# A hybrid attention and RWKV layer on one core: where the norm of half 0 keeps its tiles, and what is ordered around it

## The chip, the core and the metric

The kernel runs on one core of a Trainium2 chip. The core has a matrix engine (TensorE, called PE in the profile; PEld are its weight loads), a vector engine (DVE), a scalar engine for activations (ACT), a general engine (POOL) and a queue engine (SP) that issues the DMAs of this kernel, one after the other. The metric is the device time of one execution in microseconds (us); of several runs the median counts. Before the change it was 1794.25 us, the median of 3 runs (1792.09 to 1794.7).

## What is computed

One layer for 1024 tokens of width 1024 in fp32. Two branches, an attention with compressed, selected and windowed keys and an RWKV7 recurrence, are each projected back to width 1024, gated and added; the sum goes through an output projection onto the residual. Then comes a feed-forward block with a causal convolution of width 3 over the tokens between its two projections. Cut to what matters here:

```python
def reference(x, ...):
    h = _rms_norm(x, norm_mix[l])
    u = h @ w_in[l]
    ...
    gates = sigmoid(merge).reshape(B, S, 2, D)
    y = gates[:, :, 0] * (o_nsa @ proj_nsa[l]) + gates[:, :, 1] * (o_rwkv @ proj_rwkv[l])
    x = x + y @ w_out[l]
    x = x + _conv_ffn(_rms_norm(x, norm_ffn[l]), ffn_up[l], ffn_conv[l], ffn_down[l])

def _conv_ffn(h, w_up, conv_w, w_down):
    u = h @ w_up                                # 1024 -> 2 * 2816
    u = causal_depthwise_conv(u, conv_w)        # width 3
    a, b = jnp.split(u, 2, axis=-1)
    return (silu(a) * b) @ w_down
```

## The kernel before

Channels lie on the 128 partitions and tokens along the free axis, in two halves H[0] and H[1] of 512 tokens, so a tile is 128 x 512. A width of 1024 is eight tiles. Every fp32 operand of a large product is split into a high and a low part that the matrix engine takes as fp32r; a product of two operands is three matmuls (high by high, high by low, low by high). `wload` (L233) loads a weight tile as `wraw`, ACT copies the high part to `whi` (L240), and DVE subtracts for `wlo` (L242); there are two buffers each. `mm3` (L245) runs the three matmuls for each of `nk` tiles into one PSUM bank, one at a time (L250); `mm3s` (L254) does so for several products that share the right side (L268).

A tile framework orders the instructions of each engine. It takes them by priority, by and large in the order in which the program issues them, and lets later work of another buffer pass where an earlier one would wait; `tc.cur_priority` shifts a stretch of code back, and `tc.issue_after(i)` keeps an instruction behind instruction `i`. Each engine then runs its list strictly in order, SP's DMA issues too.

Half 0 is finished first. While the RWKV recurrence still runs, a list of dense pieces fills the matrix engine. Its tail is: `rproj` (the gated products of half 0, eight), `yprep` (splits of y), `wout0(m)` for m = 0 to 7 (L749, the output projection of half 0: 24 matmuls into bank psP; residual tile `xr` from the input, named "zs" in the profile, added at L755, stored to `x2_d` at L756, squared on ACT at L761), `norm0` (L766: two matmuls with ones that sum the squares, L770 and L771; Ln and Exp at L774 and L775; then eight tiles are loaded again from `x2_d`, scaled at L780, copied to the high part at L781 and subtracted to the low part at L782), and `ffn0(i)` for i below NEW, the FFN groups of half 0 in the plain form. A group is one 128-wide slice of both halves of `w_up`: two products of 24 matmuls. The pool "f" has three buffers of tag "zs" (NZS) and three of "fu", which the residual tiles, the squares, the reloads and other tiles share.

Half 1 follows, with later priority. `gated((m,), 1, ...)` for m = 0 to 7 makes the gated products (12 matmuls each into bank psB at L250; tanh of the gate `s` at L716; eviction at L720 on DVE; addition to y at L721 on POOL), then come splits of y (L1344, L1345), the output projection of half 1 (`project`, 24 matmuls into psA each), its norm (L1371 to L1382), with the half-0 groups i = NEW to NE - 1 as cover, and the plain FFN groups of half 1 for i below NE. Beside these, `tprep` (L1418) forms T1 to T4, sums and differences of normed tiles of the two halves (split at L1427 and L1428); `TSTEPS[i]` says which tiles' steps are issued after group i. The remaining groups, i = NE to 21, compute both halves and both slices at once as a 2 by 2 block product with seven products instead of eight (`prod`, L1528; 84 matmuls a group in place of 96). In that loop DVE builds weight sums (L1484, L1485, L1489, L1490), u2 and q from PSUM (L1557, L1562), further sums (L1565, L1570, L1574), the convolution taps (L1397, L1399) and the two multiplications of silu (L1406, L1407). FFN down ends the program.

Of the kernel before, what the change touches and what calls it, by code (L numbers as in the profile page):

```python
# [7 lines left out]
F32 = mybir.dt.float32  # L8
FR = mybir.dt.float32r
# [49 lines left out]
NE = 7  # L59
# [3 lines left out]
NEW = 5  # L63
TSTEPS = [(0,), (0, 0), (1, 1), (1, 2), (2, 2), (3, 3), (3,)]
PFD = 3
DSEQ = "nnsnsnsn"
CW = -0.5 * float(np.exp(-0.5))
# [83 lines left out]
def build(tc, D, dbg=None, upto=99):  # L151
# [7 lines left out]
    with ExitStack() as ctx:  # L159
# [84 lines left out]

        def mm3(ps, whi, wlo, xhi, xlo, nk, first=0):  # L245
            n = 0
            early = [(k, a, b) for k in range(first) for a, b in ((whi, xhi), (whi, xlo), (wlo, xhi))]
            for k, a, b in early + [(k, whi, b) for k in range(first, nk) for b in (xhi, xlo)] + [
                    (k, wlo, xhi) for k in range(first, nk)]:
                T.matmul(ps, a[:, k], ks_(b, k), start=(n == 0), stop=(n == 3 * nk - 1))  # L250
                n += 1
                yield

        def mm3s(prods, xhi, xlo, nk, lol=0):  # L254
# [10 lines left out]
            for k in range(0 if lol else nk):  # L265
# [445 lines left out]
        def gated(ms, h, hi, lo, s1, yt, pool_=None):  # L711
            ws, pj = [], []
            for m, s_ in zip(ms, s1):
                ws.append(wload(D["p_rwkv"][m], 4, pool_))
                load(s_, sg_d[8 + m][:, H[h]])
                ltanh[0] = A.activation(s_, s_, AF.Tanh, scale=0.5).ins  # L716
                pj.append(ps("PB"[h]))
            yield from mm3s(list(zip(pj, ws)), hi, lo, 4, LOL[1]) if len(ms) > 1 else mm3(pj[0], *ws[0], hi, lo, 4)
            for p_, s_, y_ in zip(pj, s1, yt):
                V.scalar_tensor_tensor(s_, s_, 1.0, p_, op0=ALU.add, op1=ALU.mult)  # L720
                G.tensor_add(y_, y_, s_)  # L721
# [27 lines left out]
        def wout0(m):  # L749
            hi, lo = wload(D["w_out"][m], 8)  # L750
            xr = FP["f"].tile([128, 512], F32, name="zs", bufs=NZS)
# [4 lines left out]
            nc.sync.dma_start(x2_d[0][m], xr)  # L756
            if m == 0:
# [8 lines left out]
        def norm0():  # L766
# [9 lines left out]
            hi, lo = ktiles(FP["h"], "hhi"), ktiles(FP["h"], "hlo")  # L776
            for k in range(8):
                t = FP["f"].tile([128, 512], F32, name=("fu", "zs")[k % 2], tag=("fu", "zs")[k % 2], bufs=(3, NZS)[k % 2])
                load(t, x2_d[0][k])
                V.scalar_tensor_tensor(t, t, P("norm_ffn", k), rs, op0=ALU.mult, op1=ALU.mult)  # L780
                A.activation(hi[k], t, AF.Copy)  # L781
                V.tensor_sub(lo[k], t, hi[k].bitcast(F32))  # L782
            ob["h2"] = hi, lo
# [3 lines left out]
        def ffn0(i, tags="PP", gate=None, evac=None):  # L787
# [8 lines left out]
            if not i:  # L796
                yield from mm3s(list(zip(pjs, ws)), *ob["h2"], 8, LOL[2])
# [1027 lines left out]
```

## Time and profile before

| | us |
|---|---|
| median of 3 runs | 1794.25 |
| the profiled execution | 1796.17 |
| its span in the trace | 1794.40 |
| PE busy | 1746.9 (97%) |
| DVE busy | 1239.4 (69%) |
| ACT busy | 864.1 (48%) |
| POOL busy | 482.0 (27%) |

The profiled execution is 1.77 us longer than the span that the trace covers, and 1.92 us longer than the median. The page of the profile has the busy time of each engine, the span in 40 slices (each digit tenths of a slice; the granted TensorE clock in tenths of full speed), the chain of work that ended last, and the costliest groups of instructions. The trace behind it gives single instructions: start, duration, engine, source line, operation, output <- inputs, shape, count, and in brackets the idle time of the engine ahead of the instruction and what released it. Matmuls overlap: the step from one start to the next, not the duration, is what one costs. The same holds in part on DVE and ACT.

### The profile page before, as it was taken

To read this page: it belongs to the slowest core of one execution; us is meant where nothing else is said; L and a number is where in the kernel's file an instruction comes from. 1 tells how busy PE (TensorE), PEld (TensorE's weight loads), DVE (VectorE), ACT (ScalarE), POOL (GpSimd) and SP (SyncE) were. 2 spreads that over 40 slices of the span, in tenths; PEclk is the share of its full clock that TensorE was granted. 3 is DMA by queue.
4 is the path that set the end of the run, shared out by engine and by line. 5 is a ranking of instruction groups with operands and counts; after the bars stand their busy time and mean duration, and the time that the engine had idled before them with its cause. 6 is when DMAs were issued, how large, how long until landed. Compare 5 with 4: busy or idle time off the path is not lost.

```text
span 1794.4 us, 30743 instructions
## 1 busy us (share of the span) xinstructions
PE 1746.9 (97%) x11849; PEld 1361.3 (76%) x11860; DVE 1239.4 (69%) x2171; ACT 864.1 (48%) x1572; POOL 482.0 (27%) x358
## 2 busy tenths in 40 slices
PE   8999999999999999999999889999999999999998
PEld 5885657676777778887777768878888888888886
DVE  6224666888776538765446475479998998876799
ACT  5234665757656654545545454355433433524330
POOL 1101031011121120000003130110454444657756
PEclk9998999999999999999999989999999999999999
DMA  6415143232344446445455663443322222524402
GB/s 193 118 53 164 54 157 108 69 110 72 109 155 140 130 141 199 137 124 160 141 159 174 232 217 118 135 145 123 114 88 89 82 77 88 204 102 130 129 13 106
DMA packets 132578, 227.03 MB, mean 127 GB/s; under 512 B 24912, under 2 KB 53968, under 8 KB 132176
## 3 DMA queue, kind: packets, MB, share of 16 engines
q1 hardware_dynamic: 132432, 225.07, 38.9%
q8 instruction: 93, 1.52, 0.4%
q14 instruction: 53, 0.43, 0.1%
HBM read 156.24 MB, written 63.96 MB: 123 GB/s over the span
## 4 chain that ended last, share of the span: by engine, by line
PE 77%; DVE 10%; DMA 5%; ACT 3%; issue 2%; POOL 1%; SPq 1%; ACTq 0%; DVEq 0%; POOLq 0%
PE psP L250 24%; PE psM L1528 7%; PE psA L1528 4%; PE psP L1528 4%; PE psA L250 4%; PE psP L268 3%; PE psB L250 2%; PE psM L250 2%; PE psA L1638 1%; PE psM L1638 1%; PE psA L444 1%; PE psB L1638 1%; PE psP L1638 1%; PE psA L583 1%; DVE pl L594 1%
## 5 line engine op out<-in xcount | busy, mean ns | idle before, releaser
L250 PE MATMUL psP<-hhi,whi 128*128 128x512 f32 x608 | 247.3, 407 | 2.7 <-DVE qn L354 1.4
L250 PE MATMUL psP<-hlo,whi 128*128 128x512 f32 x608 | 242.6, 399 | 0.5 <-DVE hlo L227 0.5
L242 DVE TENSOR_TENSOR wlo<-wraw,whi 128x1024 fp32r<-128x1024 f32 (+1 forms) x100 | 114.3, 1146 | 99.7 <-ACT whi L240 49.5
L250 PE MATMUL psP<-hhi,wlo 128*128 128x512 f32 x608 | 164.8, 402 | 0.0
L240 ACT ACTIVATE whi<-wraw 128x1024 fp32r<-128x1024 f32 (+1 forms) x100 | 95.1, 954 | 111.6 <-PE psP L250 56.4
L594 DVE TENSOR_TENSOR pl<-pf,ph 128x512 f16<-128x512 f32 (+3 forms) x208 | 113.1, 556 | 35.6 <-ACT pf L593 35.0
L250 PEld LDWEIGHTS psP<-hhi,whi 128*128 128x128 f32 x608 | 114.4, 188 | 29.3 <-ACT ad L892 1.6
L250 PEld LDWEIGHTS psP<-hlo,whi 128*128 128x128 f32 x608 | 114.4, 188 | 25.8 <-issue 2.1
L592 ACT ACTIVATE ph<-psA 128x512 f16<-128x512 f32 (+3 forms) x208 | 99.2, 477 | 65.7 <-PE psA L587 39.4
L250 PEld LDWEIGHTS psP<-hhi,wlo 128*128 128x128 f32 x608 | 112.0, 188 | 24.1 <-issue 0.5
L535 DVE TENSOR_REDUCE mp<-psM 128x1 f32<-128x512 f32 (+1 forms) x192 | 95.7, 516 | 32.8 <-PE psM L533 18.4
L593 ACT ACTIVATE pf<-psA 128x512 f32<-128x512 f32 (+3 forms) x208 | 99.6, 479 | 0.0
L1464 POOL TENSOR_TENSOR wlo<-wraw,whi 128x1024 fp32r<-128x1024 f32 (+1 forms) x31 | 63.2, 2040 | 125.4 <-DVE s L1490 59.4
L602 PEld LDWEIGHTS <-pl 128*128 128x128 f16 x592 | 55.0, 98 | 20.6 <-DVE pl L594 6.9
L616 POOL TENSOR_TENSOR onat<-onat,ot 128x256 f32<-128x256 f32 x32 | 24.5, 771 | 171.8 <-DVE ot L615 152.6
L597 PEld LDWEIGHTS <-ph 128*128 128x128 f16 x592 | 55.7, 96 | 19.4 <-issue 8.0
L1264 POOL TENSOR_TENSOR b<-b,bonus 128x512 f32<-128x512 f32 x8 | 10.4, 1294 | 205.1 <-ACT b L1262 151.9
L1407 DVE SCALAR_TENSOR_TENSOR th<-th,u 128x512 f32<-128x512 f32 x37 | 64.6, 1747 | 0.5
L1463 ACT ACTIVATE whi<-wraw 128x1024 fp32r<-128x1024 f32 (+1 forms) x37 | 32.8, 887 | 63.5 <-issue 26.8
L600 PEld LDWEIGHTS <-ph 128*128 128x128 f16 x592 | 56.1, 97 | 3.7 <-issue 3.0
L1464 POOL TENSOR_TENSOR s34l<-s,s34h 128x1024 fp32r<-128x1024 f32 x15 | 36.3, 2423 | 74.7 <-ACT s34h L1463 74.5
L1464 POOL TENSOR_TENSOR s12l<-s,s12h 128x1024 fp32r<-128x1024 f32 x15 | 37.5, 2497 | 43.1 <-PE psA L1528 31.6
(759 smaller groups left out, 5054.6 us busy)
## 6 DMA issues: line engine op xcount, KB each, us to landing
wraw<-f_up SPq DMA_DIRECT2D x58, 512.0 KB, 3.4
wraw<-w_t SPq DMA_DIRECT2D x46, 512.0 KB, 3.9
wraw<-f_dn SPq DMA_DIRECT2D x22, 512.0 KB, 3.8
th_d<-th SPq DMA_DIRECT2D x37, 256.0 KB, 2.0
sg_d<-zs SPq DMA_DIRECT2D x32, 256.0 KB, 2.9
wraw<-w_out SPq DMA_DIRECT2D x16, 512.0 KB, 3.9
z_d<-zs SPq DMA_DIRECT2D x28, 256.0 KB, 3.0
x<-xT SPq DMA_DIRECT2D x24, 256.0 KB, 5.6
```

The source lines that it names most:

```text
L240: A.activation(hi[:, :nk], raw, AF.Copy)
L242: (V if WK[0] <= wk[0] < WK[1] else G).tensor_sub(lo[:, :nk], raw, hi[:, :nk].bitcast(F32))
L250: T.matmul(ps, a[:, k], ks_(b, k), start=(n == 0), stop=(n == 3 * nk - 1))
L535: V.reduce_max(mp[:, x, br, t:t + 1], pm[:, 0:(b1 - b0) * 128], axis=AX.X)
L592: A.activation(ph[0:nkey, rg], pa[0:nkey, rg], AF.Exp, scale=0.125)
L593: A.activation(pf[0:nkey, rg], pa[0:nkey, rg], AF.Exp, scale=0.125)
L594: V.tensor_sub(pl[0:nkey, rg], pf[0:nkey, rg], ph[0:nkey, rg])
L600: T.matmul(pov[:, t, 0:64], ph[0:nkey, tk], vt[0:nkey, kb, g, 65:129], start=False, stop=False, skip_group_check=True)
L1407: V.scalar_tensor_tensor(th, th, 0.5, ub, op0=ALU.mult, op1=ALU.mult)
L1464: e.tensor_sub(lo[:, ks], raw[:, ks], hi[:, ks].bitcast(F32))
L1528: T.matmul(bank, w[wi][:, o_ + k], xs_[k][xi], start=start and n == 0, stop=n == 11, skip_group_check=True)
L1638: T.matmul(pj, x[:, m], y, start=(n == 0), stop=(n == 5))
```

## The change

Five things change. (1) The residual tiles of `wout0` get buffers of their own in the h pool (tags XT, four of them), and `norm0` works on the tiles of k = 4 to 7 where they lie; only k = 0 to 3 are loaded again. The order of the tiles is NK = 4, 5, 6, 7, 0, 1, 2, 3, in the first FFN group too. (2) On DVE, the scaling of tile n waits for the subtraction of tile n - HL, HL = 2. (3) Of the gated products of half 1, the tanh of m = 7 (GT) stands behind the last copy of the norm, the matmuls of m = 6 and 7 (GD) behind the last matmul of `wout0`, and their evictions (GE) behind the norm's last subtraction. (4) The addition to y runs on DVE instead of POOL for all m of half 1 (GV = 0). (5) NE is 6 instead of 7 and NEW 4 instead of 5: group 6 goes from the plain to the combined form, and `TSTEPS` is spread over six groups.

```diff
--- before.py
+++ after.py
@@ -56,14 +56,23 @@
 GAPS = (1, 1, 3)
 SVP = 20000
 SVI = 1
-NE = 7
+NE = 6
 WV = (3, 99, 1)
 WK = (0, 200)
 LV = 20
-NEW = 5
-TSTEPS = [(0,), (0, 0), (1, 1), (1, 2), (2, 2), (3, 3), (3,)]
+NEW = 4
+TSTEPS = [(0, 0), (0, 1), (1, 1), (2, 2), (2, 3), (3, 3)]
 PFD = 3
 DSEQ = "nnsnsnsn"
+GD = 6
+GT = 7
+GE = 6
+GV = 0
+HL = 2
+NK = (4, 5, 6, 7, 0, 1, 2, 3)
+XT = ("hhi_6", "hlo_5", "hlo_6", "hlo_7")
+HT = ("hhi_4", "hlo_4", "hhi_5", "hhi_0", "hhi_7", "hlo_0", "hhi_1", "hlo_1", "hhi_2", "hlo_2", "hhi_3", "hlo_3", "hhi_6",
+      "hlo_5", "hlo_6", "hlo_7")
 CW = -0.5 * float(np.exp(-0.5))
 LN2 = 0.6931471805599453
 
@@ -242,16 +251,18 @@
             (V if WK[0] <= wk[0] < WK[1] else G).tensor_sub(lo[:, :nk], raw, hi[:, :nk].bitcast(F32))
             return hi, lo
 
+        lastm = [None]
+
         def mm3(ps, whi, wlo, xhi, xlo, nk, first=0):
             n = 0
             early = [(k, a, b) for k in range(first) for a, b in ((whi, xhi), (whi, xlo), (wlo, xhi))]
             for k, a, b in early + [(k, whi, b) for k in range(first, nk) for b in (xhi, xlo)] + [
                     (k, wlo, xhi) for k in range(first, nk)]:
-                T.matmul(ps, a[:, k], ks_(b, k), start=(n == 0), stop=(n == 3 * nk - 1))
+                lastm[0] = T.matmul(ps, a[:, k], ks_(b, k), start=(n == 0), stop=(n == 3 * nk - 1)).ins
                 n += 1
                 yield
 
-        def mm3s(prods, xhi, xlo, nk, lol=0):
+        def mm3s(prods, xhi, xlo, nk, lol=0, ko=None):
             n = 0
             for k in range(nk if lol else 0):
                 for ps_, w_ in prods:
@@ -262,7 +273,7 @@
                 for ps_, w_ in prods:
                     T.matmul(ps_, w_[0][:, k], ks_(xlo, k), start=False, stop=(k == nk - 1))
                     yield
-            for k in range(0 if lol else nk):
+            for k in () if lol else ko or range(nk):
                 for a, b in ((0, xhi), (0, xlo), (1, xhi)):
                     for ps_, w_ in prods:
                         T.matmul(ps_, w_[a][:, k], ks_(b, k), start=(n == 0), stop=(n == 3 * nk - 1))
@@ -713,12 +724,15 @@
             for m, s_ in zip(ms, s1):
                 ws.append(wload(D["p_rwkv"][m], 4, pool_))
                 load(s_, sg_d[8 + m][:, H[h]])
-                ltanh[0] = A.activation(s_, s_, AF.Tanh, scale=0.5).ins
+                with tc.issue_after(ob["nh"]) if h and m >= GT else ExitStack():
+                    ltanh[0] = A.activation(s_, s_, AF.Tanh, scale=0.5).ins
                 pj.append(ps("PB"[h]))
-            yield from mm3s(list(zip(pj, ws)), hi, lo, 4, LOL[1]) if len(ms) > 1 else mm3(pj[0], *ws[0], hi, lo, 4)
+            with tc.issue_after(ob["wl"]) if h and ms[0] >= GD else ExitStack():
+                yield from mm3s(list(zip(pj, ws)), hi, lo, 4, LOL[1]) if len(ms) > 1 else mm3(pj[0], *ws[0], hi, lo, 4)
             for p_, s_, y_ in zip(pj, s1, yt):
-                V.scalar_tensor_tensor(s_, s_, 1.0, p_, op0=ALU.add, op1=ALU.mult)
-                G.tensor_add(y_, y_, s_)
+                with tc.issue_after(ob["nl"]) if h and ms[0] >= GE else ExitStack():
+                    V.scalar_tensor_tensor(s_, s_, 1.0, p_, op0=ALU.add, op1=ALU.mult)
+                    (V if h and ms[0] >= GV else G).tensor_add(y_, y_, s_)
 
         YS = (("fu", "fu"), ("hhi_4", "fu"), ("hhi_5", "yx"), ("hhi_0", "hlo_0"), ("hhi_1", "hlo_1"),
               ("hhi_2", "hlo_2"), ("hhi_3", "hlo_3"), ("hhi_7", "hlo_4"))
@@ -748,12 +762,14 @@
 
         def wout0(m):
             hi, lo = wload(D["w_out"][m], 8)
-            xr = FP["f"].tile([128, 512], F32, name="zs", bufs=NZS)
+            xr = FP["h"].tile([128, 512], F32, name=f"xr{m}", tag=XT[m % 4])
             load(xr, D["xT"][m][:, H[0]])
             pj = ps("P")
             yield from mm3(pj, hi, lo, ob["yh"], ob["yl"], 8, 0 if m else YE)
             V.scalar_tensor_tensor(xr, pj, 0.5, xr, op0=ALU.mult, op1=ALU.add)
             nc.sync.dma_start(x2_d[0][m], xr)
+            ob.setdefault("xr", []).append(xr)
+            ob["wl"] = lastm[0]
             if m == 0:
                 A.activation(ob["sq"], xr, AF.Square)
             else:
@@ -773,14 +789,20 @@
             rs = FP["f"].tile([128, 512], F32, name="rs0", tag="yx")
             A.activation(rs, pss, AF.Ln, bias=epst[:, 0:1], scale=1.0 / 1024)
             A.activation(rs, rs, AF.Exp, scale=-0.5)
-            hi, lo = ktiles(FP["h"], "hhi"), ktiles(FP["h"], "hlo")
-            for k in range(8):
-                t = FP["f"].tile([128, 512], F32, name=("fu", "zs")[k % 2], tag=("fu", "zs")[k % 2], bufs=(3, NZS)[k % 2])
-                load(t, x2_d[0][k])
-                V.scalar_tensor_tensor(t, t, P("norm_ffn", k), rs, op0=ALU.mult, op1=ALU.mult)
-                A.activation(hi[k], t, AF.Copy)
-                V.tensor_sub(lo[k], t, hi[k].bitcast(F32))
-            ob["h2"] = hi, lo
+            hi, lo, los = [None] * 8, [None] * 8, []
+            for n, k in enumerate(NK):
+                hi[k], lo[k] = (FP["h"].tile([128, 512], FR, name=f"h2{c}0_{k}", tag=HT[2 * n + x]) for x, c in enumerate("hl"))
+                if k > 3:
+                    t = ob["xr"][k]
+                else:
+                    t = FP["f"].tile([128, 512], F32, name=("fu", "zs")[k % 2], tag=("fu", "zs")[k % 2],
+                                     bufs=(3, NZS)[k % 2])
+                    load(t, x2_d[0][k])
+                with tc.issue_after(los[n - HL]) if n >= HL else ExitStack():
+                    V.scalar_tensor_tensor(t, t, P("norm_ffn", k), rs, op0=ALU.mult, op1=ALU.mult)
+                ob["nh"] = A.activation(hi[k], t, AF.Copy).ins
+                los.append(V.tensor_sub(lo[k], t, hi[k].bitcast(F32)).ins)
+            ob["h2"], ob["nl"] = (hi, lo), los[-1]
             for _ in range(GAPS[2]):
                 yield "gap"
 
@@ -794,7 +816,7 @@
                     yield from mm3(pjs[o], *ws[o], *ob["h2"], 8)
                     evict(i, o, pjs[o], us[o], evac)
             if not i:
-                yield from mm3s(list(zip(pjs, ws)), *ob["h2"], 8, LOL[2])
+                yield from mm3s(list(zip(pjs, ws)), *ob["h2"], 8, LOL[2], NK)
                 for o in range(2):
                     evict(i, o, pjs[o], us[o], evac)
             uv = us
```

Lines behind the diff move by 22 in the later part of the file: L1528 becomes L1550, L1557 becomes L1579.

The first place is PE around the second sum with ones, at the end of the norm's sums (sq are the added squares, zs the last square, oh and ol the RWKV output of half 1, yh the split y of half 0). Before:

```order
L250 MATMUL psP_12660<-yh6_12379,wlo_12653 128x512
L250 MATMUL psP_12660<-yh7_12383,wlo_12653 128x512
L770 MATMUL psP_12690<-sq0_12387,ones_70 128x512
L771 MATMUL psP_12690<-zs_12687,ones_70 128x512
L268 MATMUL psP_12759<-hhi_0_12696,whi_12753 128x512
L268 MATMUL psP_12767<-hhi_0_12696,whi_12761 128x512
L268 MATMUL psP_12759<-hlo_0_12704,whi_12753 128x512
```

After the change:

```order
L261 MATMUL psB_13248<-oh_13074,whi_13240 128x512
L261 MATMUL psB_13248<-ol_13075,whi_13240 128x512
L261 MATMUL psB_13248<-oh_13074,wlo_13241 128x512 x4
L787 MATMUL psP_12690<-zs_12687,ones_70 128x512
L261 MATMUL psB_13277<-oh_13074,whi_13269 128x512
L261 MATMUL psB_13277<-ol_13075,whi_13269 128x512
```

The second sum stood right behind the first and right ahead of FFN group 0; now gated products of half 1 lie on both sides of it: 24 matmuls between the two sums with ones, and 24 between the second one and FFN group 0.

The second place is DVE in the norm of half 0, from its first scaling (fu, zs and xr are the tiles scaled, hhi or h2h0 their high part). Before:

```order
L780 SCALAR_TENSOR_TENSOR fu_12712<-fu_12712,par_68,rs0_12693 128x512
L780 SCALAR_TENSOR_TENSOR zs_12717<-zs_12717,par_68,rs0_12693 128x512
L780 SCALAR_TENSOR_TENSOR fu_12722<-fu_12722,par_68,rs0_12693 128x512
L780 SCALAR_TENSOR_TENSOR fu_12732<-fu_12732,par_68,rs0_12693 128x512
L780 SCALAR_TENSOR_TENSOR zs_12727<-zs_12727,par_68,rs0_12693 128x512
L782 TENSOR_TENSOR hlo_0_12704<-fu_12712,hhi_0_12696 128x512
L780 SCALAR_TENSOR_TENSOR zs_12737<-zs_12737,par_68,rs0_12693 128x512
L782 TENSOR_TENSOR hlo_1_12705<-zs_12717,hhi_1_12697 128x512
L782 TENSOR_TENSOR hlo_2_12706<-fu_12722,hhi_2_12698 128x512
```

After the change:

```order
L802 SCALAR_TENSOR_TENSOR xr4_12544<-xr4_12544,par_68,rs0_12693 128x512
L802 SCALAR_TENSOR_TENSOR xr5_12582<-xr5_12582,par_68,rs0_12693 128x512
L1367 TENSOR_TENSOR ylo_13070<-yt_13237,yhi_13069 128x512
L804 TENSOR_TENSOR h2l0_4_12697<-xr4_12544,h2h0_4_12696 128x512
L802 SCALAR_TENSOR_TENSOR xr6_12620<-xr6_12620,par_68,rs0_12693 128x512
L804 TENSOR_TENSOR h2l0_5_12702<-xr5_12582,h2h0_5_12701 128x512
L802 SCALAR_TENSOR_TENSOR xr7_12658<-xr7_12658,par_68,rs0_12693 128x512
L804 TENSOR_TENSOR h2l0_6_12707<-xr6_12620,h2h0_6_12706 128x512
L802 SCALAR_TENSOR_TENSOR fu_12718<-fu_12718,par_68,rs0_12693 128x512
L804 TENSOR_TENSOR h2l0_7_12712<-xr7_12658,h2h0_7_12711 128x512
```

Six scalings stood ahead of most subtractions; now a subtraction follows each scaling, two tiles behind, with tiles 4 to 7 first.

The third place is DVE in the combined loop, from u2 of one group to the sum into psB (p1 and q are sums of products, u00 to u11 the four tap tiles of a group). Before:

```order
L1557 TENSOR_TENSOR u2_14962<-psM_14933,p1_14948 128x512
L1407 SCALAR_TENSOR_TENSOR th_14922<-th_14922,u10_14867 128x512
L1562 TENSOR_TENSOR q_14996<-psA_14934,p1_14948 128x512
L1399 SCALAR_TENSOR_TENSOR u11_14868<-psM_14780,par_68,u11_14868 128x2
L1407 SCALAR_TENSOR_TENSOR th_14927<-th_14927,u11_14868 128x512
L1484 TENSOR_TENSOR s12_15151<-wraw_15131 128x512
L1485 TENSOR_TENSOR s12_15151<-s12_15151,wraw_15129 128x512
L1397 SCALAR_TENSOR_TENSOR u00_15018<-psP_14932,par_68,u00_15018 128x511
L1397 SCALAR_TENSOR_TENSOR u00_15018<-psP_14932,par_68,u00_15018 128x510
L1565 TENSOR_TENSOR psB_14935<-psM_14933,q_14996 128x512
```

After the change:

```order
L1579 TENSOR_TENSOR u2_14951<-psM_14922,p1_14937 128x512
L1419 SCALAR_TENSOR_TENSOR u10_14856<-psM_14769,par_68,u10_14856 128x510
L1421 SCALAR_TENSOR_TENSOR u11_14857<-psM_14769,par_68,u11_14857 128x1
L1419 SCALAR_TENSOR_TENSOR u00_15007<-psP_14921,par_68,u00_15007 128x511
L1429 SCALAR_TENSOR_TENSOR th_14911<-th_14911,u10_14856 128x512
L1421 SCALAR_TENSOR_TENSOR u11_14857<-psM_14769,par_68,u11_14857 128x2
L1419 SCALAR_TENSOR_TENSOR u00_15007<-psP_14921,par_68,u00_15007 128x510
L1429 SCALAR_TENSOR_TENSOR th_14916<-th_14916,u11_14857 128x512
L1584 TENSOR_TENSOR q_14985<-psA_14923,p1_14937 128x512
L1587 TENSOR_TENSOR psB_14924<-psM_14922,q_14985 128x512
```

Between u2 and q there stood one multiplication of silu; now both multiplications and the taps of psP and the last of psM stand there, and the weight sums (L1484, L1485) have moved behind.

## The prediction

> **What bounds the kernel now.** I first read the page's part on the span in slices, then busy times by stretch.
>
> ```profile
> PE   8999999999999999999999889999999999999998
> PEclk9998999999999999999999989999999999999999
> 1014.00:1060.00 46.00, 41.20 (x169) 32.82 (x170) 24.27 (x31) 20.41 (x32) 16.07 (x12) 0.96 0.80 280
> 1060.00:1083.00 23.00, 15.68 (x53) 10.76 (x51) 13.52 (x21) 10.56 (x16) 0.76 (x1) 0.78 0.28 91
> 1173.00:1285.00 112.00, 111.40 (x486) 90.89 (x485) 105.46 (x164) 57.26 (x83) 20.11 (x7) 1.00 0.43 141
> 1285.00:1573.00 288.00, 288.00 (x1264) 236.85 (x1263) 258.96 (x371) 121.79 (x175) 142.83 (x69) 1.00 0.31 104
> ```
>
> A stretch row gives its length, the busy time of PE, PE's weight loads, DVE, ACT and POOL (instructions in brackets), the granted clock, the DMA share and GB/s. TensorE is the bound nearly everywhere: in 1285 to 1573, the loop in seven products, it never pauses, but DVE is busy there for 259 of 288 us. The slices have one visible dip, slices 23 and 24; in time, 1014 to 1083, where the half-0 output projection ends, half 0 is normalised and the first FFN group starts. The clock falls there too. The timeline of PE names the gaps:
>
> ```profile
> 1011.96 2.03 PE L250 MATMUL psP<-yh,wlo 128*128 128x512 f32 x8
> 1015.36 0.70 PE L250 MATMUL psB<-oh,whi 128*128 128x512 f32 x2 [1.37 <-issue]
> 1022.06 0.50 PE L250 MATMUL psP<-yh,whi 128*128 128x512 f32 x1 [3.44 <-DVE zs L755]
> 1024.31 0.63 PE L250 MATMUL psP<-yh,whi 128*128 128x512 f32 x1
> 1059.61 1.02 PE L770 MATMUL psP<-sq,ones 128*128 128x512 f32 x2
> 1062.72 1.23 PE L771 MATMUL psP<-zs,ones 128*128 128x512 f32 x2 [2.09 <-ACT zs L761]
> 1067.35 1.22 PE L268 MATMUL psP<-hhi,whi 128*128 128x512 f32 x2 [3.39 <-ACT hhi L781]
> 1069.94 1.22 PE L268 MATMUL psP<-hlo,whi 128*128 128x512 f32 x2 [1.37 <-DVE hlo L782]
> 1082.96 0.50 PE L250 MATMUL psM<-hhi,whi 128*128 128x512 f32 x1 [0.47 <-ACT whi L240]
> 1094.14 10.88 PE psP L250 x48
> ```
>
> The last row is from the chain of waits: 48 matmuls at full clock take 10.88 us, 0.2267 us each. From 1013.99 (the end of the first row, product 4 of the output projection) to 1082.96 (the second FFN group) are 68.97 us. The work in it is 72 matmuls of wout0(5) to (7), 96 of the eight gated products of half 1 and 48 of FFN group 0: 216 x 0.2267 = 49.0, and 2.2 for the two sums with ones. So 17.8 us are lost: the bracketed gaps add up to 1.37 + 3.44 + 2.09 + 3.39 + 1.37 + 0.47 = 12.1, and 5.7 are matmuls at a low clock.
>
> **Term 1, the norm of half 0.** Before, all gated products stand ahead of the end of wout0(7); nothing is left to run while the last residual, its square, the table load, Ln, Exp, scaling and split follow one another. After, 24 matmuls (products 4 and 5) stand between the two sums with ones, and 24 (6 and 7) between the second sum and FFN group 0, each 24 x 0.2267 = 5.44 us. The work is the same; only the losses change.
>
> Gap at the second sum: 2.09 under 5.44 of cover, gone. The norm chain:
>
> ```profile
> 1062.69 1.28 ACT L768 ACT_TABLE_LOAD   x1
> 1063.98 0.63 ACT L1344 ACTIVATE yhi<-yt 128x512 fp32r<-128x512 f32 x1
> 1065.88 0.75 DVE L780 SCALAR_TENSOR_TENSOR fu<-fu,par,rs 128x512 f32<-128x512 f32 x1 [0.55 <-ACT rs L775]
> 1066.66 0.63 ACT L781 ACTIVATE hhi<-fu 128x512 fp32r<-128x512 f32 x1 [0.82 <-DVE fu L780]
> ```
>
> From the end of the second sum (1063.95) to the first FFN matmul are 3.4 us now. The change puts on ACT, between Exp and the first split, a table load (1.28, the tanh of product 6 needs another table), that tanh (0.63) and one split of y, so about 0.5 more that DVE's scaling doesn't hide: 5.8 against 5.44. I take 0.7 with the lag of the second tile; the gap at L782 (1.37) goes, as subtractions alternate with scalings. Bounds: 0 if ACT slips the tanh in while DVE scales, 3.0 if each 128x512 step on ACT lands late. In the Trainium skill, "ScalarE: Activation LUTs", section "What ACT_TABLE_LOAD costs", a drain of about 1.38 us follows each load, which speaks against an added load. This trace shows none: the load at 1062.69 is followed by work at 1063.98, 1.29 later. By that rule the forecast would be an estimated 1785.4.
>
> Start of the stretch. The residual tiles no longer share the three "zs" buffers, so their loads move up in SP's queue and wout0(5) follows wout0(4) without the 1.37. What comes late next is the weight tile of wout0(6):
>
> ```profile
> 1015.98 5.31 DMA zs<-xT
> 1016.65 0.33 SPq L157 DMA_DIRECT2D wraw<-w_out  x1
> 1023.22 1.06 ACT L240 ACTIVATE whi<-wraw 128x1024 fp32r<-128x1024 f32 x1 [0.48 <-DMA wraw<-w_out]
> ```
>
> It is split at 1024.3. wout0(5) and one gated product (36 matmuls) last until 1013.99 + 8.16 = 1022.15: 2.1 idle instead of 3.44 and 1.37. Does a gap of 2.1 cool the clock?
>
> ```profile
> 945.00:950.00 5.00, 2.81 (x34) 1.92 (x32) 2.48 (x6) 1.89 (x3) 0.00 (x0) 0.76 0.55 189
> 947.30 1.02 PE L268 MATMUL psP<-ohi,whi 128*128 128x512 f32 x2 [2.19 <-ACT ohi L704]
> 1015.00:1020.00 5.00, 3.26 (x12) 2.10 (x12) 2.05 (x3) 2.15 (x4) 0.00 (x0) 1.00 1.06 398
> ```
>
> A gap of 2.19 stands at a clock of 0.76, one of 1.37 at 1.00; so yes, and by the row at 1024.31 (0.42 from one matmul to the next) some eight matmuls cost 1.5. The Trainium skill, "TensorE: Matmul & The Clock Gate", section "Part 1: The HAM clock gate", sets the idle window at about 3.4 us. The trace has a low clock beside 2.19; by the rule the 1.5 would fall away and the forecast be an estimated 1782.5.
>
> The loss at 1082.96 (0.5) stays, since the next group's weights wait for the same buffers. For loads that come later in SP's queue (four reloads of x2 fewer, but weights and gates in another order) I add 1.0. Bounds 0 and 5.7, all of today's low-clock loss again, since DMA is at 0.80 in this stretch.
>
> New losses: 2.1 + 1.5 + 0.7 + 0.5 + 1.0 = 5.8 instead of 17.8: **-12.0**, bounds -17.3 (only the 0.5 left) and -5.
>
> The y addition of half 1 moves from POOL to DVE, eight times 0.6. DVE has 24.27 of 46 us busy; the two last evictions wait for the norm's last subtraction, and behind them on DVE stand only splits for matmuls 48 and more later. I cost it at 0; without that cover 1.2.
>
> **Term 2, one FFN group.** A group in both halves takes 96 matmuls plain and 84 combined: -12 x 0.2267 = **-2.7**. PE is bound on both sides, so this counts in full.
>
> **Term 3, the way into the combined loop.** The plain groups of half 1 cover DVE's sums T1 to T4.
>
> ```profile
> 1024.31 1.23 DVE L242 TENSOR_TENSOR wlo<-wraw,whi 128x1024 fp32r<-128x1024 f32 x1 [2.30 <-ACT whi L240]
> 1025.45 0.68 DVE L1334 TENSOR_TENSOR ol<-stg,oh 128x512 fp32r<-128x512 f32 x1
> 1182.14 5.39 DVE L1378 SCALAR_TENSOR_TENSOR hf<-x,par,rstd 128x512 f32<-128x512 f32 x8 [1.12 <-ACT rstd L1373]
> 1272.51 0.39 PE L1528 MATMUL psP<-hhi,whi 128*128 128x512 f32 x1
> 1277.84 0.20 DVE L1399 SCALAR_TENSOR_TENSOR u<-cvl,par,u 128x1 f32<-128x1 f32 x1
> 1279.36 0.67 DVE L1428 TENSOR_TENSOR T2l<-t,T2h 128x512 fp32r<-128x512 f32 x1
> 1280.73 0.39 PE L1528 MATMUL psM<-T2l,s12h 128*128 128x512 f32 x1
> 1284.27 0.50 PE L1528 MATMUL psM<-T2h,s12h 128*128 128x512 f32 x1 [0.60 <-ACT s12h L1463]
> ```
>
> The last T2 tile is done at 1280.03 and used at 1280.73: 0.7 of slack, with DVE busy 105.46 of 112. One plain half-1 group less takes 48 matmuls (10.9) from PE's way there; T2's last tile is wanted seven matmuls later in the loop (+1.6): 9.3 earlier. DVE, by the two orders from the first L1378 to that T2l, loses four taps (0.66), two 1024-wide splits (1.14 from start to start) and four small ones (0.13) and gains two 512-wide (0.60): 4.2. PE waits 9.3 - 4.2 - 0.7 = 4.4, with 0.7 for the clock after it (some four matmuls at 0.42), less the 0.60 that is there now: **+4.5**. Bounds 0 (DVE's 6.5 us of idle time lie where it can use them) and 6.5 (the same again for T1 and T4).
>
> **Sum.** -12.0 - 2.7 + 4.5 = -10.2. The profiled execution took 1796.17 (span 1794.40 and 1.77 around it): 1786.0. It lies 1.9 above the median of the runs shown, 1794.25, so I predict **1784.0**. All good ends give -20 (1774), all bad ones -1.2 (1793).
>
> **Rivals.** *The loop waits for DVE* (the other side). The scheduler also orders the combined groups, sixteen after the change, in another way:
>
> ```profile
> 1438.13 0.68 DVE L1562 TENSOR_TENSOR q<-psA,p 128x512 f32<-128x512 f32 x1
> 1442.26 0.39 PE L1528 MATMUL psA<-h2hi,s34h 128*128 128x512 f32 x1
> 1455.08 2.28 DVE L1407 SCALAR_TENSOR_TENSOR th<-th,u 128x512 f32<-128x512 f32 x1
> ```
>
> q must be read before the h2 product may add to psA: 3.4 us of slack now. After, two taps, two small ones and a second 2.28 us multiply come ahead of q, 4.4 later; the h2 product comes 26 matmuls after T1's end instead of 12, 3.2 later. That leaves 2 us, and DVE is busy there for 258.96 of 288, 17.2 us of a group's 19.1 (84 x 0.2267). For each us that DVE runs later than this, all sixteen groups pay: 16 us. From 0.64 us beyond (10.2 / 16) the kernel is no faster than before; 1 us beyond gives 1784 + 16 = 1800. Against it: nothing is added per group, and PE never waits in this loop now. Chance 0.08.
>
> *Loads bind the norm stretch*: the DMA row for the gates,
>
> ```profile
> s<-sg_d SPq DMA_DIRECT2D x8, 256.0 KB, 5.4
> ```
>
> lands slowly, and products 6 and 7, now last, wait for gates and weights behind SP's queue. Then term 1 gives only 5: 1791. Chance 0.15. Should the gated products at the end only move the wait (the norm starts 5.4 us later), it is the same price.
>
> *No wait at the loop's entry*: DVE uses its idle time, term 3 is 0 or nearly, 1779 to 1780. Chance 0.17. My forecast keeps 0.60.
>
> **How the numbers follow.** The range takes in the forecast, the no-wait rival and most of the load rival: 1776 to 1792. A measurement can tell about 0.2% (3.6 us) from no change. Faster by more than that (under 1790.7): 0.60 + 0.17 and a little of the load rival, 0.80; within it 0.12; slower than 1797.8: 0.08.
>
> **What would show it.** In the changed profile the second sum with ones follows gated matmuls without a gap; FFN group 0 starts with under 1 us idle; the second FFN group comes some 57 us after wout0(4) instead of 69; one gap of about 2 us stands before wout0(6) with ACT's split of w_out behind it; the loop's entry has one PE wait of about 4 us on a T tile from DVE; PE is busy without pause afterwards, 19.1 us a group. Gaps in every group before psA's h2 product, or idle time before products 6 and 7 put down to a DMA, would prove me wrong.

## The result and the profile after

The changed kernel took 1781.18 us (median of 20 runs, 1775.68 to 1794.13) against 1795.39 us of the kernel before in the same series (20 runs, 1785.96 to 1803.52). The ratio is 0.9925, 95% interval 0.9907 to 0.9943; it is estimated from all runs of both kernels, and so differs a little from the quotient of the two medians (0.9921). Two later comparisons of the same kernel gave 0.9936 (0.9913 to 0.9960; medians 1785.49 against 1794.33) and 0.9934 (0.9912 to 0.9956; 1781.15 against 1793.13). 1784.0 was forecast.

The page's two lines on PE in the 40 slices, after:

```profile
PE   8999999999999999999999999999999999999998
PEclk9998999999999999999999999999999999999999
```

The dip in slices 23 and 24 is gone, and in this view so is the low clock beside it; a slice is 44.5 us long and hides a cold stretch of 6 us that is left (see the timeline below). The waits of PE from 980 us on, after (engine, line, releaser; us in all, times, longest):

```profile
PE psP L261 <- ACT whi L249: 4.3, 1, 4.3
PE psP L1660 <- DVE acc L1740: 1.3, 1, 1.3
PE psP L1550 <- ACT p L1576: 1.2, 1, 1.2
PE psM L261 <- ACT whi L249: 1.1, 1, 1.1
PE psM L1550 <- DVE T2l L1450: 0.4, 1, 0.4
```

None of them is in the norm: the waits at the sums and at the first FFN group have left the list. One wait is larger than any before, 4.3 us on a weight split; two small ones stand at the entry of the combined loop. The timeline of PE around the norm, after:

```profile
1023.59 0.80 PE L261 MATMUL psP<-yh,whi 128*128 128x512 f32 x1 [4.30 <-ACT whi L249]
...
1045.81 1.02 PE L786 MATMUL psP<-sq,ones 128*128 128x512 f32 x2
1052.13 1.02 PE L787 MATMUL psP<-zs,ones 128*128 128x512 f32 x2
1058.61 0.73 PE L279 MATMUL psP<-h2h,whi 128*128 128x512 f32 x2
1071.26 0.50 PE L261 MATMUL psM<-h2h,whi 128*128 128x512 f32 x1 [1.12 <-ACT whi L249]
```

The second sum comes 6.3 us after the first and FFN group 0 another 6.5 us later, with no idle time: 24 gated matmuls run in each of these stretches. After the wait of 4.30, 14 matmuls start 0.43 us apart instead of 0.23, up to 1029.72: the clock is low there.

Three lengths serve for all runs below. **w0** is the start of the first matmul of wout0(0). **S** is the time from w0 to the first matmul of the second FFN group, less 29.87, the time from w0 to the end of wout0(4) in the trace before (1013.99 - 984.12). So S is the stretch that the prediction has at 68.97. **E** runs from there to the end of the last matmul; it holds terms 2 and 3. All are read from the start times of single matmuls.

| kernel | w0 | S | E | wait for wout0(6)'s weights | waits at FFN group 0 | ratio to before, 95% interval |
|---|---|---|---|---|---|---|
| before | 984.1 | 69.0 | 707.3 | (3.4 on the residual tile) | 4.8 | 1 |
| changed | 981.1 | 60.3 | 706.7 | 4.3 | 0 | 0.9925, 0.9907 to 0.9943 |
| changed, again | 977.2 | 58.0 | 708.8 | 3.0 | 0.2 | 0.9936, 0.9913 to 0.9960 |
| changed, third | 979.0 | 58.9 | 706.1 | 3.3 | 0.8 | 0.9934, 0.9912 to 0.9956 |
| norm's part alone | 985.8 | 58.7 | 706.8 | 3.6 | 0.3 | 0.9930, 0.9908 to 0.9952 |
| FFN group alone | 977.7 | 71.2 | 707.0 | (3.4 on the residual tile) | 4.3 | 1.0014, 0.9992 to 1.0037 |
| zs buffers, reload | 977.6 | 63.9 | 706.7 | (3.5 on the residual tile) | 2.9 | 0.9978, 0.9958 to 0.9997 |
| no holds | 982.8 | 60.7 | 708.9 | 3.1 | 2.6 | 0.9952, 0.9934 to 0.9971 |
| no lag | 977.2 | 62.1 | 708.1 | 3.0 | 3.7 | 0.9936, 0.9914 to 0.9958 |
| additions on POOL | 984.1 | 60.9 | 706.1 | 3.4 | 1.6 | 0.9951, 0.9933 to 0.9969 |
| x loads late | 979.3 | 53.7 | 708.8 | 0 | 1.4 | 0.9905, 0.9874 to 0.9936 |
| x loads late, second time | 982.7 | 53.4 | 708.8 | 0 | 1.0 | 0.9905, 0.9882 to 0.9929 |
| x and y late | 980.8 | 55.5 | 706.7 | 0 | 1.6 | 0.9927, 0.9903 to 0.9952 |
| first combined product early | 981.5 | 53.7 | 715.2 | 0 | 1.4 | 0.9975, 0.9953 to 0.9997 |

Between the first two traces the span fell by 1794.4 - 1781.9 = 12.5. Of this 8.7 is S and 0.7 is E; 3.0 lie ahead of w0, and 0.1 at the very end. The 3.0 are not the change's: w0 lies anywhere from 977.2 to 985.8, in kernels whose program up to there is the same, and at 981.1, 977.2 and 979.0 in three traces of one and the same kernel.

### The profile page after: what moved, and what is told of

Read it like the earlier page. It is cut to its first block, busy times and chain, and to the rows that moved or that the text cites. A ratio compares the mean times of both kernels' runs of the same rounds, so it can differ in the third digit from the quotient of the medians.

```text
span 1781.9 us, 30738 instructions
## 1 busy us (share of the span) xinstructions
PE 1739.7 (98%) x11837; PEld 1355.8 (76%) x11848; DVE 1240.7 (70%) x2184; ACT 869.4 (49%) x1572; POOL 480.0 (27%) x354
## 4 chain that ended last, share of the span: by engine, by line
PE 78%; DVE 11%; DMA 5%; ACT 3%; issue 2%; SPq 1%; POOL 0%; DVEq 0%; ACTq 0%; POOLq 0%
PE psP L261 24%; PE psM L1550 7%; PE psA L1550 5%; PE psP L1550 5%; PE psA L261 4%; PE psB L261 3%; PE psP L279 2%; PE psM L261 2%; PE psA L1660 1%; PE psM L1660 1%; PE psA L455 1%; PE psB L1660 1%; PE psP L1660 1%; PE psA L594 1%; DVE pl L605 1%
## 5 line engine op out<-in xcount | busy, mean ns | idle before, releaser
L261 PE MATMUL psP<-hhi,whi 128*128 128x512 f32 x560 | 228.7, 408 | 2.7 <-DVE qn L365 1.4
L261 PE MATMUL psP<-hlo,whi 128*128 128x512 f32 x560 | 224.0, 400 | 0.5 <-DVE hlo L236 0.5
L261 PE MATMUL psP<-hhi,wlo 128*128 128x512 f32 x560 | 152.7, 403 | 0.0
L261 PEld LDWEIGHTS psP<-hhi,whi 128*128 128x128 f32 x560 | 105.4, 188 | 27.5 <-ACT ad L914 1.6
L261 PEld LDWEIGHTS psP<-hlo,whi 128*128 128x128 f32 x560 | 105.4, 188 | 24.0 <-issue 1.9
L261 PEld LDWEIGHTS psP<-hhi,wlo 128*128 128x128 f32 x560 | 103.0, 188 | 22.2 <-issue 0.5
L1486 POOL TENSOR_TENSOR wlo<-wraw,whi 128x1024 fp32r<-128x1024 f32 (+1 forms) x33 | 68.0, 2060 | 143.0 <-PE psA L261 46.3
L1429 DVE SCALAR_TENSOR_TENSOR th<-th,u 128x512 f32<-128x512 f32 x38 | 59.6, 1567 | 0.1
L1485 ACT ACTIVATE whi<-wraw 128x1024 fp32r<-128x1024 f32 (+1 forms) x38 | 33.5, 880 | 42.4 <-PE psP L1550 28.6
L1550 PE MATMUL psP<-h2h,whi 128*128 128x512 f32 x128 | 50.1, 391 | 1.2 <-ACT p L1576 1.2
```

Of the source, the lines that this page charges most:

```text
L261: lastm[0] = T.matmul(ps, a[:, k], ks_(b, k), start=(n == 0), stop=(n == 3 * nk - 1)).ins
L1429: V.scalar_tensor_tensor(th, th, 0.5, ub, op0=ALU.mult, op1=ALU.mult)
L1486: e.tensor_sub(lo[:, ks], raw[:, ks], hi[:, ks].bitcast(F32))
L1550: T.matmul(bank, w[wi][:, o_ + k], xs_[k][xi], start=start and n == 0, stop=n == 11, skip_group_check=True)
```

## The experiments

**The norm's part alone.** The changed kernel with the old numbers of groups.

```diff
-NE = 6
+NE = 7
-NEW = 4
+NEW = 5
-TSTEPS = [(0, 0), (0, 1), (1, 1), (2, 2), (2, 3), (3, 3)]
+TSTEPS = [(0,), (0, 0), (1, 1), (1, 2), (2, 2), (3, 3), (3,)]
```

> The changed kernel with NE = 7, NEW = 5 and the old TSTEPS: the norm's part alone. S is the stretch from the end of wout0(4) to the first matmul of the second FFN group, 68.97 us before and 60.31 in the changed kernel. Theory (the norm's part gives most of the gain): S 60 to 61, the wait for wout0(6)'s weights about 4, no gap at the sums; loop entry as before (0.6); the time 8 to 12 below before, ratio 0.9935 to 0.9955. Rival (the 3 us that already separate the two traces ahead of wout0 come from the change too): the same S, but 11 to 13 below before, ratio under 0.9935.

S 58.7, a wait of 3.6, ratio 0.9930, that is 12.5 us of 1792.67 with an interval from 9 to 16. S is a little under what the theory gave. The ratio lies in the rival's range, and its interval takes in the theory's as well. But its trace has w0 at 985.8, later than in the kernel before, so the new norm gains nothing ahead of wout0; and the next run, with the old norm, has w0 at 977.7. The norm's part carries the gain; the rival falls with w0.

**The FFN group alone.** The kernel before with the new numbers.

```diff
-NE = 7
+NE = 6
-NEW = 5
+NEW = 4
-TSTEPS = [(0,), (0, 0), (1, 1), (1, 2), (2, 2), (3, 3), (3,)]
+TSTEPS = [(0, 0), (0, 1), (1, 1), (2, 2), (2, 3), (3, 3)]
```

> The kernel before with NE = 6, NEW = 4 and the new TSTEPS: one FFN group moved to the combined form, the norm untouched. As forecast: 12 matmuls fewer (-2.7), a wait at the loop's entry of 4 to 5: +1.8, ratio 1.001. Theory after the trace (DVE uses its idle time, entry costs about 2.3): -0.4, ratio 0.9998, entry gaps 1 to 2 in all. Rival (the entry costs nothing): -2.7, ratio 0.9985. S stays 69 in all three.

Ratio 1.0014 (0.9992 to 1.0037), E 707.0 against 707.3: the time cannot tell the forecast (1.001) from the theory (0.9998), and the rival's 0.9985 lies just outside. The trace gives -0.3 and one wait at the entry. The timeline of PE and a stretch behind the wait (length, PE, PEld, DVE, ACT, POOL, PEclk, DMA share, GB/s), this kernel:

```profile
1254.17 0.50 PE L1528 MATMUL psP<-hhi,whi 128*128 128x512 f32 x1 [1.22 <-ACT p L1554]
1255.00:1260.00 5.00, 5.00 (x16) 3.93 (x15) 4.97 (x10) 1.75 (x2) 1.08 (x1) 0.66 0.15 57
```

So twelve matmuls fewer (2.7) are nearly given back at the entry: the wait is 0.6 longer than the one there before, and behind it seven matmuls start 0.43 us apart at a low clock, which costs 1.4. In the changed kernel's first trace the same wait of 1.22 stands at the same place, and the clock stays at 1.00. S is 71.2 here where 69 was expected: its gaps are those of the kernel before, 0.4 longer in all (3.0 instead of 2.1 at the second sum), and most of the rest are more matmuls at a low clock.

**Residual tiles in the shared buffers again**, with all eight loaded again. The holds (GD, GT, GE) and the lag (HL) stay.

```diff
-            xr = FP["h"].tile([128, 512], F32, name=f"xr{m}", tag=XT[m % 4])
+            xr = FP["f"].tile([128, 512], F32, name="zs", bufs=NZS)
...
-                if k > 3:
+                if k > 8:
```

> The changed kernel with the residual tiles back in the shared zs buffers and all eight tiles loaded again for the norm; the three holds and the lag stay. Theory (the buffers decide where the gated products stand, and these products are the cover): all eight products run ahead of the sums again, gaps of about 2 at the second sum and about 3 at the first FFN matmul return, S 66 to 70, the whole 6 to 9 slower than the changed kernel. Rival (the holds alone keep two products back, and the lag helps): the gap at the first FFN matmul stays under 1, S 62 to 64.

The timeline of PE, this kernel:

```profile
1008.42 0.70 PE L261 MATMUL psB<-oh,whi 128*128 128x512 f32 x2 [0.97 <-issue]
1015.12 0.50 PE L261 MATMUL psP<-yh,whi 128*128 128x512 f32 x1 [3.45 <-DVE zs L769]
...
1052.70 1.02 PE L786 MATMUL psP<-sq,ones 128*128 128x512 f32 x2
1053.55 1.02 PE L787 MATMUL psP<-zs,ones 128*128 128x512 f32 x2
1057.46 1.22 PE L279 MATMUL psP<-h2h,whi 128*128 128x512 f32 x2 [2.89 <-ACT h2h L803]
```

Neither case as written. The wait ahead of FFN group 0 (2.89) returns, as the theory said, and so does the wait for the residual tile (3.45), which it did not name; but the second sum follows the first at once, since the holds alone keep products 6 and 7 behind wout0, where they cover the last square. S is 63.9, in the rival's band, 3.6 to 5.8 above the changed kernel's three traces and 5.1 under before. So by S the buffers of the residual tiles are worth about half of the gain. By the ratios (0.9978 against 0.9925 to 0.9936) it is more, 7.5 to 9.5 us, but each of these ratios has an interval of some 4 us to either side. The buffers bring 24 of the 48 covering matmuls to their place and start wout0(5) without a wait.

**No holds.**

```diff
-GD = 6
-GT = 7
-GE = 6
+GD = 8
+GT = 8
+GE = 8
```

> The changed kernel with GD, GT and GE = 8, so no hold of the tanh, the matmuls or the evictions of products 6 and 7. Theory (the buffers decide, the holds do little): the products stay where they are on PE, S 60 to 62, the time within 2 us of the changed kernel. Rival (the holds keep DVE and ACT free for the norm): two evictions and two additions (2.4) and a tanh run ahead of the norm's tiles, a gap of 1.5 to 3 at FFN group 0, S 62 to 64.

```profile
1059.39 0.74 PE L279 MATMUL psP<-h2h,whi 128*128 128x512 f32 x2 [1.58 <-ACT h2h L803]
1061.98 0.72 PE L279 MATMUL psP<-h2l,whi 128*128 128x512 f32 x2 [0.19 <-DVE h2l L804]
1064.45 0.73 PE L279 MATMUL psP<-h2l,whi 128*128 128x512 f32 x2 [0.81 <-DVE h2l L804]
```

In this PE timeline the matmuls of the products stand where they did (sums 6.3 apart, FFN group 0 after 24 more), but 1.58 + 0.19 + 0.81 = 2.6 of waits come at FFN group 0, as the rival said. S is in the theory's band all the same; it grows by less (60.7 against 58.0 to 60.3), because the waits ahead of it came out smaller in this trace: 3.1 for wout0(6) and 0.5 for the second group. The holds place no matmul here; what they do is keep DVE and ACT free for the norm's tiles.

**No lag.**

```diff
-HL = 2
+HL = 8
```

> The changed kernel with HL = 8: DVE scales all eight tiles ahead of the first subtraction. Theory (the alternation brings the low parts in time): the first low part comes 6 x 0.66 = 4 later; FFN group 0 takes it as its third matmul, so a gap of 2.5 to 4 at it, S 62.5 to 65. Rival (the tiles follow faster afterwards, the lag only evens it out): gap under 1.4, S under 62.

```profile
1052.10 0.73 PE L279 MATMUL psP<-h2h,whi 128*128 128x512 f32 x2
1056.54 1.22 PE L279 MATMUL psP<-h2l,whi 128*128 128x512 f32 x2 [3.71 <-DVE h2l L804]
```

The gap is 3.71, between the first high part and the first low part, as the theory had it; S 62.1, 0.4 under its band. Beside the second trace of the changed kernel (S 58.0, with the same 3.0 for wout0(6)) it costs 4.1. The ratio (0.9936) does not show that: 4 us of 1790 are 0.0022, the width of its interval to one side.

**Additions to y on POOL.**

```diff
-GV = 0
+GV = 8
```

> The changed kernel with the additions to y of half 1 on POOL again (1.3 to 1.7 each there, 0.6 on DVE). As forecast (the move costs and gives nothing): S 58 to 60.5, the gap at FFN group 0 under 0.5, within 1 us of the changed kernel. Rival (on ACT the split of product 5's y stands ahead of the norm's first copy and waits for POOL): a gap of 0.7 to 2 at FFN group 0, S 60 to 62.

S 60.9 and 1.14 + 0.47 at FFN group 0: the rival's size. Its reason is another, as ACT's timeline shows:

```profile
1056.13 1.28 ACT L790 ACT_TABLE_LOAD   x1
1057.43 0.69 ACT L790 ACTIVATE rs<-psP,epst 128x512 f32<-128x512 f32 x1
1058.13 1.28 ACT L791 ACT_TABLE_LOAD   x1
1059.43 0.63 ACT L791 ACTIVATE rs<-rs 128x512 f32<-128x512 f32 x1
1059.97 0.61 ACT L1366 ACTIVATE yhi<-yt 128x512 fp32r<-128x512 f32 x1
```

The split of y (L1366) waits for nothing. The scheduler has put two tanh ahead of Ln, and a table load now stands ahead of Ln and another ahead of Exp, both between the second sum and the norm's tiles. Why the order came out so is not shown.

**The x loads late.** In the changed kernel the largest wait is for the weights of wout0(6). SP's issues, after:

```profile
1011.61 0.33 SPq L166 DMA_DIRECT2D x<-xT  x1
1012.29 0.32 SPq L770 DMA_DIRECT2D x_d<-xr  x1
1013.01 0.33 SPq L166 DMA_DIRECT2D wraw<-p_rwkv  x1
1013.65 0.33 SPq L166 DMA_DIRECT2D x<-xT  x1
1014.33 0.33 SPq L770 DMA_DIRECT2D x_d<-xr  x1
1015.01 0.33 SPq L166 DMA_DIRECT2D wraw<-w_out  x1
```

ACT's split of these weights, and two stretches of the same trace:

```profile
1022.48 1.06 ACT L249 ACTIVATE whi<-wraw 128x1024 fp32r<-128x1024 f32 x1 [5.51 <-DMA wraw<-w_out]
```

```profile
1010.00:1015.00 5.00, 5.00 (x24) 4.05 (x23) 2.06 (x4) 3.01 (x5) 0.20 (x1) 1.00 1.01 370
1015.00:1020.00 5.00, 4.29 (x19) 3.15 (x17) 1.80 (x3) 1.26 (x2) 1.49 (x1) 1.00 1.05 403
```

The load is issued at 1015.01 behind the loads of half 1 and its data come 7.4 us later, with DMA full. SP itself waits too; two of its waits for landings between 1004 and 1020 us (us in all, times, longest):

```profile
SPq L166 <- DMA wraw<-p_rwkv: 2.3, 3, 1.8
SPq L166 <- DMA s<-sg_d: 1.5, 2, 1.2
```

The DMAs of this trace use eight semaphores in turn, and none is issued before the one eight issues ahead of it has landed: the issue at 1015.01 follows the landing, at 1014.99, of the load issued at 1008.64. So every transfer that stands ahead in SP's list delays a load twice, at its issue and on its way. The tiles x are wanted only when half 1's output projection is added. The edit:

```diff
             hi, lo = wload(D["w_out"][m], 8)
+            if m == 6:
+                ob["ww"] = lastw[0]
...
-            with tc.issue_after(lastw[0]):
+            with tc.issue_after(lastw[0]), tc.issue_after(ob["ww"]) if m < 4 else ExitStack():
                 load(x2[m], D["xT"][m][:, H[1]])
```

> The changed kernel with the four first loads of half 1's residual (x, 1 MB) issued behind the weights of wout0(6). Theory (the 4.3 us wait is the weights standing behind these loads in SP's queue while DMA is full): at about 380 GB/s the weights land 2.8 earlier, the wait falls to 0.5 to 2 and the cold clock behind it goes, S 54 to 57, 4 to 6 us faster than the changed kernel. Rival (another load binds, the wait moves to wout0(7) or a product): S 59 to 62, no gain.

SP and ACT, this kernel:

```profile
1008.79 0.33 SPq L166 DMA_DIRECT2D wraw<-w_out  x1
1009.47 1.67 SPq L166 DMA_DIRECT2D x<-xT  x3
```

```profile
1014.75 1.06 ACT L249 ACTIVATE whi<-wraw 128x1024 fp32r<-128x1024 f32 x1 [1.93 <-DMA wraw<-w_out]
```

The split starts at 1014.75 instead of 1022.48, 7.7 earlier: 1.8 is w0, 4.4 the earlier issue (1008.79), 1.5 the shorter way of the data (5.9). The wait is gone, the clock stays at 1.00, and S is 53.7: better than the theory's 2.8 us of DMA time, and the weights of a gated product have moved behind those of wout0(6) as well. A wait of 1.0 at FFN group 0, with 0.4 behind it, is new beside the first trace; here too the table loads stand ahead of Ln and Exp.

**x and y late.** In addition the last two splits of y wait for the split of the second FFN group's weights (`lasta[0]`, kept as `ob["w1"]`, is that split on ACT; the lines that keep it are left out here).

```diff
-            A.activation(yhi[:, m], yt, AF.Copy)
+            with tc.issue_after(ob["w1"]) if m >= GE else ExitStack():
+                A.activation(yhi[:, m], yt, AF.Copy)
```

> The same, and the splits of y for products 6 and 7 on ACT stand behind the split of the second FFN group's weights. Theory (that split waits in ACT's order behind a split of y that waits for DVE's held evictions): the wait at the second FFN group falls from 1.1 to 0.5, S 0.6 below the kernel with the late x loads. Rival (the weights wait for their buffer): unchanged.

A miss: the wait at the second group is 0.47, but it is 0.47 without this edit too, once the x loads are late. S is 55.5, longer by 1.8, with a clock of 0.87 in FFN group 0 (1053 to 1066 us). What makes the 1.1 of the changed kernel was thus not tested. ACT's rows there, in the changed kernel, fit the theory, no more:

```profile
1069.63 0.63 ACT L1366 ACTIVATE yhi<-yt 128x512 fp32r<-128x512 f32 x1 [0.74 <-DVE yt L735]
1070.17 1.04 ACT L249 ACTIVATE whi<-wraw 128x1024 fp32r<-128x1024 f32 x1
```

**The first combined product early**, on top of the late x loads. At the entry ACT stands like this in the changed kernel:

```profile
1242.22 0.69 ACT L1416 ACTIVATE u<-psB,par 128x512 f32<-128x512 f32 x1 [3.96 <-DVE th L1429]
...
1244.89 0.62 ACT L1449 ACTIVATE T4h<-t 128x512 fp32r<-128x512 f32 x1
1245.59 0.63 ACT L1427 ACTIVATE th<-u 128x512 f32<-128x512 f32 x1
1246.13 0.58 ACT L1576 ACTIVATE p<-psP 128x512 f32<-128x512 f32 x1
```

The copy p of the first product is ready to run when that product ends (about 1241.7), and stands behind a tap (u) that waited 3.96 for DVE, and behind the splits of T1 to T4.

```diff
             pa, pb, pc, pd_ = ps("P"), ps("M"), ps("A"), ps("B")
+            pr_ = tc.cur_priority
+            if i == NE:
+                tc.cur_priority = pr_ - 300
             prod(pa, w["a"], 0, b11, True)
             p1 = tmp("p1", "zs", NZS)
             A.activation(p1, pa, AF.Copy)
+            if i == NE:
+                tc.cur_priority = pr_
```

> The kernel with the late x loads, and the first combined group's first product and its copy p1 on ACT taken 300 steps earlier in priority. Theory (the wait of 1.2 at the loop's entry is p1 standing in ACT's order behind the last T splits, which wait for DVE): that wait goes, the loop's entry (first L1550-type matmul after the last plain group to the end of the program, with the 12 matmuls that move ahead counted) costs 1 to 2 less, 1776 to 1777, ratio 0.988 to 0.991. Rival (DVE binds whatever ACT's order): the wait comes back a few matmuls later on a T tile with the same 1 to 3 us in all, the time as with the late x loads alone.

```profile
1245.77 0.79 PE L1552 MATMUL psA<-T1l,s12h 128*128 128x512 f32 x1 [4.18 <-DVE T1l L1452]
...
1313.64 0.50 PE L1552 MATMUL psA<-h2hi,s34h 128*128 128x512 f32 x1 [1.83 <-DVE q L1591]
```

The rival, and worse: E grows by 6.4 to 715.2, ratio 0.9975. The waits at the entry with the late x loads alone, 1.5 on T1 and 1.2 on p, became one of 4.18 on T1 from DVE; then the loop waits for q, five times, 2.7 in all, and 0.8 for p of a later group. DVE is the bound at the entry (in the changed kernel it is busy without pause from 1225 to 1250 us); who is served first there decides where PE waits, and here it waits longer, 7.7 in all instead of 2.7. These waits ahead of the h2 product are the prediction's slower rival, in another kernel.

**Both once more, side by side.**

> The kernel with the late x loads again, beside the changed kernel, since its interval overlapped. Theory (its stretch S is 4 to 6 shorter): S 53 to 55, no wait for wout0(6)'s weights, ratio 0.989 to 0.992 and 0.002 to 0.0035 under the changed kernel's beside it. Rival (the gain is given back elsewhere): S the same but the ratios within 0.001 of each other.

> The changed kernel a third time. S 58 to 61, the wait for wout0(6)'s weights 3 to 4.5, ratio 0.992 to 0.994; loop entry in one of the two forms seen so far (539.1 or 541.2 from the first combined matmul to the end).

0.9905 (0.9882 to 0.9929) and 0.9934 (0.9912 to 0.9956): 0.0029 apart, the first time 0.0031. The intervals overlap, but S, 53.4 and 53.7 against 58.0 to 60.3, does not. By the ratios the late x loads beat the changed kernel by some 5 us and the kernel before by 17 us. By S and E together they are 3.9 us ahead of the changed kernel's mean: both traces have the longer E, 708.8, which the changed kernel has in one of three. The changed kernel's second trace was expected to have S at 59 to 62 and had 58.0, and a w0 near 981 if the 3 us ahead of wout0 came from the change; it was 977.2.

## Why the prediction was right, and where not

The sum was -10.2. The three traces of the changed kernel and the one of the norm's part have S at 58.0 to 60.3, mean 59.0; the two with the old norm have 69.0 and 71.2: **term 1 is -11.1**, forecast -12.0. (Against the one trace of the kernel before alone, the changed kernel's three give -8.7, -11.0 and -10.1.) E is 707.1 in the two traces with seven plain groups and 707.5 on the mean of the eleven others that keep the loop's entry as it is (706.1 to 708.9): **terms 2 and 3 together +0.4**, forecast +1.8. Together -10.7. The measured ratios say -13.5 (-16.7 to -10.2), -11.5 and -11.8, so the sum of the terms lies inside each interval, in the first at its edge; the median of 1781.18 lies 2.8 under the forecast.

Term 1, step by step. The gaps at the sums and at the low parts are gone, as forecast. Giving the residual tiles shared buffers again takes 24 covering matmuls from their place and brings 2.9 back; taking away the lag brings 3.7 back, taking away the holds 2.6. So cover and order are the causes and not company. That tiles 4 to 7 come first was not tested by itself. The norm chain against its 24 matmuls left 0, 0.2 and 0.8, forecast 0.7. The added table load stands where the forecast put it, between Exp and the first split, and cost no drain; ACT's timeline, after:

```profile
1055.48 1.28 ACT L728 ACT_TABLE_LOAD   x1
1056.88 0.63 ACT L728 ACTIVATE s<-s 128x512 f32<-128x512 f32 x1
```

The tanh follows 1.40 after the load's start, and at the earlier load of this norm (1050.74) a weight split follows 1.30 after it.

The mechanism that comes late next, the weights of wout0(6), was named rightly but undersized: 2.1 forecast, 4.3, 3.0 and 3.3 measured. The step that was off is that I kept the split of these weights 10.3 us after the end of wout0(4) (1024.3 - 1013.99). It hangs on the loads of half 1 that stand ahead in SP's queue, and was done 11 to 13 us after it. The clock after this wait cost more in the first trace, 14 matmuls at about 0.43 (3.0); in the other two it was eight (1.6), as I had it (1.5). The 1.0 for other late loads was not needed, and the second FFN group waited 1.1 instead of 0.5. So term 1 gave less than forecast, and terms 2 and 3 cost less. That the two nearly cancel is luck, and 0.5 between forecast and account is less than what S alone varies by between traces of one kernel (2.3).

Term 2 holds: 96 matmuls left one side and 84 came back. Term 3 is mis-sized: 3.1 by E (0.4 + 2.7) against 4.5. I had one wait of 4.4 on a T tile from DVE. There are one to three: most often 1.6 in all (1.22 on p, 0.42 on T2l) or 2.7 (1.5 on T1h, 1.22 on p). Most sit on ACT, whose queue hands DVE's lateness on, and one of 0.6 stood there before. In five of the eleven traces, among them the changed kernel's second, six to eight matmuls at a low clock follow (1.4 to 1.7), in the other six none; I had four (0.7). So the step that was off is the wait, which I had too long and on the wrong engine; the clock came out on both sides of mine.

The rivals: the loop's new order left q enough room here.

```profile
1445.84 0.68 DVE L1584 TENSOR_TENSOR q<-psA,p 128x512 f32<-128x512 f32 x1
```

It ends at 1446.5, and the h2 product of that group starts at 1450.34: 3.8 of slack, where the prediction had 2 left. (The prediction speaks of two taps that come ahead of q; the order shows three, and its 4.4 fits three.) That loads would bind the norm's stretch came true in small: one wait for one load, 3 to 4 us, of which the forecast itself had 2.1; not the whole 7.

## What to carry to other kernels

Where a serial chain (square, sum, Ln, Exp, scale, split) stands between two large products, count its length and put just so many independent matmuls behind its start; what decides whether a scheduler can do so is often the buffers that the chain's tiles share, and then the queue of the loads behind them. A load's place in that queue counts from its issue on: here each issue waited for the transfer eight before it. After such an edit look for the next load in the DMA queue ahead of which something stands that nobody waits for; moving four loads back was worth another 4 to 5 us here. Where the bound engine's queue feeds the others, look twice before taking an operation out of line on another engine: here that moved the wait and made it longer.

## What the runs showed of the hardware

With the DMA engines full (1.01 and 1.05 of them, 370 and 403 GB/s, from 1010 to 1020 us in the changed kernel), transfers of mostly 256 KB landed 0.6 to 0.7 us apart, and a 512 KB load took 7.4 us instead of the page's median of 3.5. SP's issues came 0.6 to 0.7 us apart too; this is not SP's own pace but the eight semaphores: each issue waited for a landing.

A pause well under the 3.4 us that the Trainium skill gives as the idle window ("TensorE: Matmul & The Clock Gate", "Part 1: The HAM clock gate") was enough for a low clock here: after a wait of 3.00, in the changed kernel's second trace, the clock was 0.69 from 1020 to 1025 us. By that rule no cold matmuls would have followed; the trace does not agree. The length of the pause alone does not decide either: after a wait of 1.22 at the loop's entry the clock was 0.66 with the FFN group alone (1255 to 1260 us), and 1.00 after the same wait in the changed kernel's first trace (1245 to 1255 us). What decides is not shown.

The same work ahead of wout0 ended anywhere from 977.2 to 985.8 us over the traces, and 3.9 us apart in three traces of one kernel, more than several of the effects here: stretches of the trace between fixed instructions resolved what the times could not.
